# Hard-max attention on one core: dots without their pause late on, a third step in the last tiles, a larger allowance for value-row gathers, five rows ahead of the last flags

## The chip, the cores and the metric

The kernel runs on one core of one Trainium2 chip. The metric is device time in microseconds, 443.18 us before the change (median of three, 442.71 to 443.21). The profile is of one execution with a span of 441.9 us, and its times count from the start of the span. The five engines are PE (matrix), ACT (scalar), DVE (vector), POOL (GpSimd, which here issues nearly all gathers) and SP (which issues stores).

## The reference

```python
# q, k, v: (4, 4096, 128) float32
logits = np.matmul(q, k.transpose(0, 2, 1))
best = np.argmax(logits, axis=-1)
b_idx = np.arange(q.shape[0])[:, None]
return v[b_idx, best, :].astype(np.float32)
```

For each of 16384 query rows the kernel finds the key with the largest dot product, and returns that key's row of v.

## The kernel before

**Tiles.** There are 4 batches of 32 query tiles, T = 128 tiles of 128 queries. A loop over `it` handles them in a software pipeline. The order of instructions on each engine is written out by hand (a manual schedule), so each engine runs its list in the order in which the Python code emits it.

**Screen.** For each tile PE forms scores of groups of four keys in fp16, with ACT turning two 1024-wide blocks into absolute values (A, L234) and one into integers (E, L247). The DVE `fold` (L260) joins the blocks into W, which carries a group index in its low bits, and `top` (L264) takes the eight best of W. In iteration `it`, `fold` handles tile `it - 1` and `top` tile `it - 2`.

**Candidates and dots.** `gather` (L271) extracts the best group of four or two tiles (cand, L276) and puts one indirect DMA per tile into the list `near_q` (kg, L282): differences of the four keys of that group. When these are issued, a generator `dots` (L290) multiplies them with the queries (prod L300), halves twice (L305, L308) and reduces (L310). A generator advances one operation per call of `step`, of which there are two in an iteration, one after `fold` and one after `top`. A yielded `("wait", 1)` makes it pause to the next iteration; `("dve",)` lets it go on at the next step. Tiles below 108 go in groups of four, later ones in groups of two.

**Picks and rows.** When all dots of a chunk (eight tiles, four from tile 96 on) are there, `pick` (L313) finds which of the four keys wins. Its last operation is win (L333). `put_values` (L337) then puts one gather per tile (vr from v, L342) into the list `late_q`, and behind each four a store to the output (L346), which SP issues.

**The issue of gathers.** At the end of each iteration `issue` (L743) sends to POOL first what is due of `near_q`, then one of the list `fast` (gathers of the flag check), and then rows of `late_q` as long as an allowance `room` lasts. That grows by `rate` per iteration, is capped at 3, and is lowered by what was issued and by loads (`busy`).

**The end.** After the loop come the last dots and picks. `flags_last` (L466) recomputes exactly the few queries whose screen was too close: DVE makes the list of rows (row_e, L509), POOL issues `LATE` of the waiting value rows (L515), then gathers three groups of keys and the query (FK, FQ, L512); DVE computes exact dots (L594) and the winner xw_fe (L607). The other waiting rows go out by `late(1 << 20)` (L531), then the gather FV of the exact winner's row (L540), and last the scatter of FV to the output (L541), which must come after all stores to it. An earlier check of the same kind, `flag_segment` (L358), handles the first half of the tiles inside the loop.

Of the kernel before, what the change touches and what calls it, by code (L numbers as in the profile page):

```python
# [21 lines left out]
TAU = 8.0  # L22
NEAR = 0.5
SLOTS = 6
LATE = 4
NKG = 6


# [1 line left out]
def kernel(ctx, tc, q, k, v, out):  # L30
# [5 lines left out]
    T = B * NQT  # L36
# [34 lines left out]
    def put_k(b, h):  # L71
        if b >= B:
            return
        src = natk[b % 2][:, h].rearrange("p (g f) d -> p g f d", f=4)
        nc.vector.tensor_tensor(out=kd[:, h], in0=src[:, :, 1:4, :], in1=src[:, :, 0:1, :].to_broadcast([P, 4, 3, P]),
                                op=OP.subtract)
        kb16 = k16[b].rearrange("(h p n) d -> p h (n d)", p=P, n=16)
        nc.sync.dma_start(out=kb16[:, h], in_=kd[:, h].rearrange("p g f d -> p (g f d)"))
# [10 lines left out]
    def add_rest(b, h):  # L89
        if b >= B:  # L90
            return
        src = natk[b % 2][:, h].rearrange("p (g f) d -> p g f d", f=4)
        kb16 = k16[b].rearrange("(r x) d -> r (x d)", x=4).rearrange("(h p g) (f d) -> p h g f d", h=2, p=P, f=3)
        nc.gpsimd.dma_start(out=kb16[:, h].rearrange("p g f d -> p g (f d)"), in_=src[:, :, 1:4, :].rearrange("p g f d -> p g (f d)"),
                            accum_op=OP.add)

    def load_part(b, i, n=8):
        if b >= B:
            return
        if i < 8:  # L100
            load_k(b, i // 4, i % 4 * 4, i % 4 * 4 + n)
        else:
            load_q(b, (i - 8) * NQT // 8, (i - 8 + n // 4) * NQT // 8)
# [103 lines left out]
    def turn_q(b, x, y):  # L207
        nc.sync.dma_start_transpose(out=qT[b % 2][:, x * P:y * P].rearrange("p (t r) -> p t r", r=P),
                                    in_=natq[b % 2][:, x:y, :].rearrange("p t d -> p (t d)"))
# [42 lines left out]
    def screen(t):  # L252
        dpart(t, 0)
        spart(t - 1, 0)
        dpart(t, 1)
        spart(t - 1, 1)

    def fold(t):
        E, ps = E_t.pop(t)
        nc.vector.scalar_tensor_tensor(out=W_t[t % NW].bitcast(I16)[:, 1::2], in0=ps, scalar=QSCALE, in1=E,  # L260
                                       op0=OP.mult, op1=OP.max)
# [28 lines left out]
    def dots(c, x, m):  # L290
        c0 = chunks[c][0]
        d = D_t[c % 4]
        b = x // NQT
        gap = ("wait", 1) if m == 4 and x < 200 else ("dve",)
        yield "until", lambda: ("kg", x) in done, 2 if m < 4 and x < TAIL else 1
        kg = kg_t.pop(x)
        prod = rp.tile([P, 4, 3, P], FP16, tag="prod", name=f"prod_{x}")[:, 0:m]
        h = min(m, 2)
        for i in range(0, m, h):
            nc.vector.tensor_tensor(out=prod[:, i:i + h], in0=kg[:, i:i + h],  # L300
                                    in1=natq[b % 2][:, x + i - b * NQT:x + i + h - b * NQT, :].unsqueeze(2).to_broadcast([P, h, 3, P]),
                                    op=OP.mult)
            yield gap
        p1 = rp.tile([P, 4, 3, 64], FP16, tag="p1", name=f"p1_{x}")[:, 0:m]
        nc.vector.tensor_tensor(out=p1, in0=prod[:, :, :, 0:64], in1=prod[:, :, :, 64:128], op=OP.add)  # L305
        yield gap
        p2 = rp.tile([P, 4, 3, 32], FP16, tag="p2", name=f"p2_{x}")[:, 0:m]
        nc.vector.tensor_tensor(out=p2, in0=p1[:, :, :, 0:32], in1=p1[:, :, :, 32:64], op=OP.add)  # L308
        yield "dve",
        nc.vector.tensor_reduce(out=d[:, x - c0:x - c0 + m, 1:4], in_=p2, axis=AX_X, op=OP.add)  # L310
        done.update(("dot", i) for i in range(x, x + m))
# [154 lines left out]
    def flags_last(t0, t1, ready, fill, late):  # L466
# [44 lines left out]
        def get(dst, src, idx, hi):  # L511
            nc.gpsimd.indirect_dma_start(out=dst, out_offset=None, in_=src, in_offset=IOA(ap=idx, axis=0),  # L512
                                         bounds_check=hi - 1, oob_is_err=False)

        late(LATE)  # L515
        get(FK[:, 0, :], k_flat, gb[:, 0:1], B * Sk)
# [173 lines left out]
    def ready(s, it):  # L690
        if s["until"] is not None:
            if not s["until"]():
                return False
            s["until"], s["wake"] = None, it + s["n"]
        return it >= s["wake"]

    def advance(s, it, free):
        if not (ready(s, it) or free and s["until"] is None):
            return False
        try:  # L700
            y = next(s["g"])
        except StopIteration:
            live.remove(s)
            return True
        if y[0] == "wait":
            s["wake"] = it + y[1]
        elif y[0] == "until":
            s["until"], s["n"] = y[1], y[2]
            return advance(s, it, free)
        return True  # L710

    def step(it):
        quick = it >= TAIL
        waiting = [s for s in live if s["kind"] == "dots" and ready(s, it)]
        quota = 2 if len(waiting) > 1 else 1
        again = []
        for s in list(live):
            if s["kind"] == "dots":
                if quota and advance(s, it, False):
                    quota -= 1  # L720
            elif advance(s, it, False) and (quick or s["kind"] == "flags"):
                again.append(s)
        for s in again:
            if s in live:
                advance(s, it, False)
# [3 lines left out]
    def take_late(n):  # L729
        while n > 0 and late_q:  # L730
            g = late_q.pop(0)
            n -= g not in stores
            g()
        while late_q and late_q[0] in stores:
            wait_q.append((clock[0] + 2, late_q.pop(0)))
# [3 lines left out]
    def put_out(now):  # L739
        while wait_q and wait_q[0][0] <= now:  # L740
            wait_q.pop(0)[1]()

    def issue(it):  # L743
        n = 0
        clock[0] = it
        put_out(it)
        behind = len([g for g in near_q if g not in marks]) > (2 if it >= TAIL else 4)
        while near_q and (n < 1 + behind or near_q[0] in marks or it >= T - 1):
            g = near_q.pop(0)
            n += g not in marks  # L750
            g()
        if fast and it >= rest[0]:
            fast.pop(0)()
            rest[0] = it + 2
            n += 1
        if it < 16:
            take_late(2 if n == 0 and len(late_q) > 4 else 1)
            return
        b, qt = it // NQT, it % NQT
        busy = 0.7 if qt % 2 == 0 and (10 <= qt < 18 and b + 1 < B or 18 <= qt < 26 and b + 2 < B) else 0.0  # L760
        if qt in (13, 17) and b + 1 < B:
            busy += 1.0
        rate = 2.42 if it < 72 else 2.5 if it < 100 else 2.42
        room[0] = min(room[0] + rate - busy, 3.0) - n
        for i in range(2):
            if room[0] >= 1 and late_q and it < T - 1:
                take_late(1)
                room[0] -= 1
# [20 lines left out]
    for b in range(1, B):  # L789
        x = b * NQT  # L790
        units += [(x - 1, x - NQT + (6 + 3 * i // 2 if b == 1 else 1 + 2 * i), unit_k, b, i) for i in range(16)]
    for it in range(T):
        b, qt = it // NQT, it % NQT
        if it < 8:
            load_part(1, it, 4)
        elif 10 <= qt < 18 and qt % 2 == 0:
            load_part(b + 1, qt - 2)
        elif 18 <= qt < 26 and qt % 2 == 0:
            load_part(b + 2, qt - 18)
        open_units = [u for u in units if u[1] <= it]  # L800
        if open_units:
            u = min(open_units)
            units.remove(u)
            assert it <= u[0]
            u[2](*u[3:])
        if it == 1:
            turn_q(0, 4, 8)
        if it == 40:
            nc.sync.dma_start(out=q32, in_=q[B - 1].rearrange("(p t) d -> p t d", p=P)[:, NQT - 2:NQT])
        if it in (1, 2, 3):  # L810
            turn_q(0, it * 8, it * 8 + 8)
        elif qt >= 16 and qt % 2 == 0 and b + 1 < B:
            turn_q(b + 1, (qt - 16) * 2, (qt - 14) * 2)
        if it > 0:
            screen(it)
        if it >= 1:
            fold(it - 1)
        if it == 1:
            put_k(0, 1)
        if it % NQT in (9, 13):  # L820
            put_first(it // NQT + 1, it % NQT // 13)
        if it % NQT in (13, 17):
            add_rest(it // NQT + 1, it % NQT // 17)
        step(it)
        if it >= 2:
            top(it - 2)
        step(it)
        if it >= 2:
            gathers(it - 2)
        issue(it)  # L830
# [75 lines left out]
```

## Time and profile before

| What | Value |
|---|---|
| time, median of 3 | 443.18 us |
| span of the profile | 441.9 us |
| main loop, start of the last L264 | 405.5 us |
| kg gathers L282 on POOL | 126, 1003 ns each |
| vr gathers L342 with win as index | 126, 999 ns each |
| fold L260 on DVE | 128, 1306 ns |
| L264 on DVE | 128, 1227 ns |
| landing after issue, kg and vr | 3.0 and 2.7 us (medians) |

A group line of the profile gives the line, engine, operation, the tile written and the tile read, the count, the summed busy time and the mean of one. Consecutive DVE instructions overlap a little, so the distance between their starts is shorter than the duration (1.20 against 1.31 us for the fold). A gather's bar on POOL covers its issue alone; the data land later.

From the chain of work that ended last, its lines by share of the span, and its final part (start, length, engine, what):

```profile
ACT A L234 31%; ACT E L247 6%; DVE TOP L264 4%; PE psn L225 4%; POOL vr L342 4%; PE pd L225 4%; POOL kg L282 4%; DVE W L260 4%; PE psn L244 3%; DMA vr<-in_v_dram,win 3%; DMA natk<-in_k_dram 2%; DMA out_dram<-vr 1%; DMA kg<-k,cand 1%; DVE prod L300 1%; DMA vr<-in_v_dram,win_w 1%
...
419.83 2.60 DMA FK<-in_k_dram,gb_e
422.43 5.59 DMA vr<-in_v_dram,win
429.02 1.00 POOL vr L342
430.32 1.00 POOL vr L342
431.62 3.17 DMA vr<-in_v_dram,win_w
434.88 1.82 DMA out_dram<-vr
437.46 1.25 POOLq L901
```

### The profile page before, as it was taken

How to read it: one execution, taken by the hardware profiler on the slowest of the kernel's cores; microseconds unless marked ns; L12 is line 12 of the kernel's file. 1: busy time of each engine (PE TensorE's matmuls, PEld its weight loads, DVE VectorE, ACT ScalarE, POOL GpSimd, SP SyncE). 2: the span in 40 equal slices, each digit the busy share in tenths (PEclk: the TensorE clock that was granted, in tenths of full speed). 3: DMA queues.
4: the chain of work that ended last, by engine and by line, in shares of the span. 5: the costliest groups of instructions: out<-in, count | busy, mean ns of one | idle time of the engine just before them, and what ended most of it. 6: DMA issues, size and time to landing. Idle time of an engine off the chain costs nothing.

```text
span 441.9 us, 6163 instructions
## 1 busy us (share of the span) xinstructions
PE 378.9 (86%) x1830; PEld 168.0 (38%) x1830; DVE 405.9 (92%) x734; ACT 375.6 (85%) x437; POOL 306.2 (69%) x335
## 2 busy tenths in 40 slices
PE   7999999999999999999998889999889997892100
PEld 4444444444444444444443334443333333330100
DVE  2688999999999999999999999999999999999840
ACT  2899999999999999999998889999989998892000
POOL 8413456677768786777777776777777777777673
PEclk9999999999999999999999999999999999998555
DMA  7933999463326999743336993453322332323432
GB/s 123 202 101 65 157 148 139 106 130 80 108 58 134 180 163 170 147 114 91 84 94 142 173 162 100 96 132 107 85 82 84 90 89 80 88 80 102 122 113 53
DMA packets 52868, 50.54 MB, mean 114 GB/s; under 512 B 34136, under 2 KB 40890, under 8 KB 52832
## 3 DMA queue, kind: packets, MB, share of 16 engines
q0 software_dynamic: 19072, 33.87, 39.2%
q1 hardware_dynamic: 33760, 16.26, 14.5%
q8 instruction: 14, 0.23, 0.2%
q14 instruction: 22, 0.18, 0.2%
HBM read 40.05 MB, written 14.55 MB: 124 GB/s over the span
## 4 chain that ended last, share of the span: by engine, by line
ACT 37%; issue 20%; DVE 13%; PE 12%; POOL 8%; DMA 8%; POOLq 0%; ACTq 0%; DVEq 0%; SPq 0%
ACT A L234 31%; ACT E L247 6%; DVE TOP L264 4%; PE psn L225 4%; POOL vr L342 4%; PE pd L225 4%; POOL kg L282 4%; DVE W L260 4%; PE psn L244 3%; DMA vr<-in_v_dram,win 3%; DMA natk<-in_k_dram 2%; DMA out_dram<-vr 1%; DMA kg<-k,cand 1%; DVE prod L300 1%; DMA vr<-in_v_dram,win_w 1%
## 5 line engine op out<-in xcount | busy, mean ns | idle before, releaser
L234 ACT ACTIVATE A<-pd 128x1024 f16<-128x1024 f32 x256 | 260.8, 1046 | 12.5 <-PE pd L225 12.0
L282 POOL DMA_INDIRECT kg<-k,cand x126 | 126.4, 1003 | 80.0 <-DVE cand L276 48.7
L260 DVE SCALAR_TENSOR_TENSOR W<-psn,E 128x1024 int16<-128x1024 f32 x128 | 167.1, 1306 | 7.4 <-ACT E L247 5.3
L225 PE MATMUL psn<-kT,qT 128*128 128x512 f16 x512 | 151.9, 378 | 11.4 <-ACT A L234 4.0
L225 PE MATMUL pd<-kT,qT 128*128 128x512 f16 x512 | 151.9, 379 | 8.7 <-ACT A L234 8.2
L264 DVE MAX8 TOP<-W 128x8 f32<-128x1024 f32 x128 | 157.0, 1227 | 0.0
L225 PEld LDWEIGHTS <-qT 128*128 128x128 f16 x1024 | 97.9, 97 | 151.8 <-issue 62.0
L342 POOL DMA_INDIRECT vr<-in_v_dram,win x126 | 125.9, 999 | 40.0 <-issue 36.1
L244 PE MATMUL psn<-A,identh 128*128 128x512 f16 x512 | 152.1, 378 | 0.0
L247 ACT ACTIVATE E<-psn 128x1024 int16<-128x1024 f32 x128 | 132.6, 1036 | 2.3 <-PE psn L244 1.5
L244 PEld LDWEIGHTS <-identh 128*128 128x128 f16 x512 | 49.6, 97 | 60.7
L300 DVE TENSOR_TENSOR prod<-kg,natq 128x768 f16<-128x768 f16 x63 | 34.8, 554 | 0.4 <-DMA kg<-k,cand 0.4
L205 ACT ACTIVATE kT<-uk 128x256 f16<-128x256 f32 x48 | 20.6, 429 | 1.5 <-PE uk L202 1.5
L305 DVE TENSOR_TENSOR p<-prod 128x768 f16<-128x768 f16 (+1 forms) x36 | 18.1, 502 | 0.1
L310 DVE TENSOR_REDUCE D<-p 128x12 f32<-128x384 f16 (+1 forms) x36 | 17.7, 492 | 0.1
L201 PE MATMUL uk<-identh,natk 128*128 128x128 f16 x96 | 15.8, 218 | 0.0
L484 PE MATMUL fp_e<-n_e,tri 128*128 128x1 f32 x2 | 0.6, 364 | 13.5 <-DVE n_e L482 13.5
L202 PEld LDWEIGHTS <-natk 128*128 128x128 f16 x96 | 9.3, 97 | 7.2 <-issue 5.1
L308 DVE TENSOR_TENSOR p<-p 128x384 f16<-128x384 f16 (+1 forms) x36 | 11.9, 330 | 0.1
L66 POOL DMA_DIRECT2D natk<-in_k_dram x19 | 11.3, 599 | 0.8 <-POOLq L890 0.8
L201 PEld LDWEIGHTS <-natk 128*128 128x128 f16 x96 | 9.3, 98 | 5.6
L69 POOL DMA_DIRECT2D natq<-in_q_dram x15 | 9.2, 614 | 0.0
(152 smaller groups left out, 140.1 us busy)
## 6 DMA issues: line engine op xcount, KB each, us to landing
out_dram<-vr SPq DMA_DIRECT2D x31, 256.0 KB, 2.1
natq<-in_q_dram POOLq DMA_DIRECT2D x12, 256.0 KB, 5.3
natk<-in_k_dram POOLq DMA_DIRECT2D x10, 256.0 KB, 4.5
k<-kd SPq DMA_DIRECT2D x18, 128.0 KB, 3.7
k<-natk POOLq DMA_DIRECT2D x6, 384.0 KB, 6.4
kg<-k,cand POOLq DMA_INDIRECT x126, 3.0
vr<-in_v_dram,win POOLq DMA_INDIRECT x126, 2.7
natk<-in_k_dram POOLq DMA_DIRECT2D x8, 128.0 KB, 5.7
```

The source lines that it names most:

```text
L201: nc.tensor.matmul(out=o, lhsT=natk[b % 2][:, h, 4 * m + x, :], rhs=identh, start=True, stop=False)
L205: nc.scalar.activation(out=kT[b % 2][:, c:c + 256], in_=ps, func=AF.Copy)
L225: nc.tensor.matmul(out=ps[:, n * 512:(n + 1) * 512], lhsT=qT[b % 2][:, qt * P:(qt + 1) * P], rhs=kT[b % 2][:, u * 1024 + n * 512:u * 1024 ...
L234: nc.scalar.activation(out=A, in_=ps, func=AF.Abs)
L244: nc.tensor.matmul(out=ps[:, n * 512:(n + 1) * 512], lhsT=identh, rhs=A[:, n * 512:(n + 1) * 512], start=False, stop=True)
L247: nc.scalar.activation(out=E, in_=ps, func=AF.Relu, scale=QSCALE)
L260: nc.vector.scalar_tensor_tensor(out=W_t[t % NW].bitcast(I16)[:, 1::2], in0=ps, scalar=QSCALE, in1=E, op0=OP.mult, op1=OP.max)
L264: nc.vector.max(out=TOP[:, t, :], in_=W_t[t % NW].bitcast(FP32))
L282: near_q.append(lambda j=j: nc.gpsimd.indirect_dma_start(out=kg[:, j].rearrange("p f d -> p (f d)"), out_offset=None, in_=k16[t0 // NQT], ...
L300: nc.vector.tensor_tensor(out=prod[:, i:i + h], in0=kg[:, i:i + h], in1=natq[b % 2][:, x + i - b * NQT:x + i + h - b * NQT, :].unsqueeze(2 ...
L305: nc.vector.tensor_tensor(out=p1, in0=prod[:, :, :, 0:64], in1=prod[:, :, :, 64:128], op=OP.add)
L342: late_q.append(lambda j=j: nc.gpsimd.indirect_dma_start(out=vr[:, j, :], out_offset=None, in_=v_flat, in_offset=IOA(ap=win[:, i + j:i + j ...
```

## The change

Four edits are meant to shorten the queue of value rows that is still waiting when the loop ends. Dots of tile 80 and later no longer pause a tile between operations, so that they take two steps a tile. In the last 20 iterations there is a third step. The allowance is raised by stages. And five instead of four rows go out ahead of the last flags' gathers.

```diff
-LATE = 4
+LATE = 5
...
-        gap = ("wait", 1) if m == 4 and x < 200 else ("dve",)
+        gap = ("wait", 1) if m == 4 and x < 80 else ("dve",)
...
-        rate = 2.42 if it < 72 else 2.5 if it < 100 else 2.42
+        rate = 2.45 if it < 72 else 2.65 if it < 80 else 2.45 if it < 96 else 2.6 if it < 104 else 2.45 if it < 112 else 2.6
...
         if it >= 2:
             top(it - 2)
         step(it)
+        for _ in range(1 if it >= T - 20 else 0):
+            step(it)
         if it >= 2:
             gathers(it - 2)
         issue(it)
```

## The prediction

> **What bounds the kernel now.** I read the windows first, then the waits of GpSimd, then the timeline of the end. First the busy times of the engines, as totals and in two late stretches (columns: window, length, then busy time and count of PE, PEld, DVE, ACT, POOL, then clock, DMA share, GB/s):
>
> ```profile
> PE 378.9 (86%) x1830; PEld 168.0 (38%) x1830; DVE 405.9 (92%) x734; ACT 375.6 (85%) x437; POOL 306.2 (69%) x335
> ...
> 330.00:360.00 30.00, 28.07 (x118) 11.32 (x117) 29.86 (x52) 28.70 (x31) 22.69 (x23) 1.00 0.30 83
> 360.00:390.00 30.00, 26.10 (x110) 10.47 (x109) 29.55 (x60) 25.82 (x28) 22.36 (x22) 1.00 0.32 92
> ```
>
> DVE is busy 29.86 and 29.55 of 30 us: up to the last L264 (405.5 us) the time is the sum of DVE's work. One tile costs it 1.20 us for the fold L260 plus 1.14 for L264 (start to start), and dots, candidates and picks bring four tiles to some 12.2 us. POOL looks 75% busy, but is nearly full too:
>
> ```profile
> POOL vr L342 <- issue: 7.2, 22, 0.8
> POOL kg L282 <- issue: 4.6, 15, 0.3
> POOL kg L282 <- DVE cand L276: 2.9, 5, 0.9
> ```
>
> These are POOL's waits from 347 to 405 us: 0.30 us of "issue" before each gather, so a gather occupies POOL 0.95 to 1.00 + 0.30, about 1.27 us, and true waiting for a candidate is only 2.9 us, 0.3 of each being that same gap. At 3.05 us a tile POOL fits 2.4 gathers a tile, two of which would suffice for one kg and one vr; the rest works off the backlog. And the backlog decides the end (timeline):
>
> ```profile
> 411.38 0.16 DVE L333 SCALAR_TENSOR_TENSOR win<-CNT,cand 128x4 uint32<-128x4 f32 x1
> ...
> 413.88 1.00 POOL L342 DMA_INDIRECT vr<-in_v_dram,win  x1 [0.30 <-issue]
> ...
> 417.17 1.05 POOL L512 DMA_INDIRECT FK<-in_k_dram,gb_e  x1 [2.29 <-DVE row_e L509]
> ...
> 421.13 1.00 POOL L512 DMA_INDIRECT FK<-in_k_dram,gb_e  x1 [0.31 <-issue]
> ...
> 422.43 1.00 POOL L342 DMA_INDIRECT vr<-in_v_dram,win  x1 [0.30 <-issue]
> ...
> 426.57 0.17 DVE L607 TENSOR_REDUCE xw_fe<-xl_fe 128x1 uint32<-128x12 f32 x1
> ...
> 431.62 1.00 POOL L342 DMA_INDIRECT vr<-in_v_dram,win_w  x1 [0.30 <-issue]
> 432.92 0.99 POOL L512 DMA_INDIRECT FV<-in_v_dram,xw_fe  x1 [0.30 <-issue]
> 437.69 1.02 POOL L541 DMA_INDIRECT out_dram<-FV,rowk_e  x1 [3.77 <-DMA out_dram<-vr]
> ```
>
> After the four flag gathers (417.17 to 422.1) eight value rows still stand in POOL's queue, 422.43 to 432.6, one every 1.30 us. Only then come FV (its index was ready at 426.74) and, after the last store has landed, the scatter. From 422 us on POOL is the bound. Ahead of FK it waited 2.29 us for DVE.
>
> **What the skill says.** "Perfetto Trace Analysis", section "DMA Instruction — SWDGE (GPSIMD)": a GpSimd DMA's bar ends when the descriptors are written, not when the data are there. The trace agrees: 1.00 us bars, median landing 2.7 us after issue for vr and 3.0 for kg. "DMA: Bandwidth & Descriptors", section "Anatomy of one DMA — SWDGE (gpsimd) path", gives about 2.0 us plus bytes over 436 GB/s; for a kg gather of 96 KB that makes 2.2 us, an estimate by the page, and the trace's 3.0 is what I use. No page prices the reordering itself.
>
> **The change part by part.** No instruction is added or removed; I compared the order on each engine in the two built programs. I number gathers by tile: k112 is the kg gather of tile 112, v112 its value row.
>
> *Dots without the one-tile pause (x from 80), third step in the last 20 tiles.* On DVE the same operations stand earlier. DVE is saturated, so its sum is unchanged: 0. The picks come earlier: adding up the DVE durations ahead of each L333, its win moves forward 4.1 us for the picks of tiles 80 to 103, 6.5 to 7.2 for those of 104 to 111, 3.1 for 112 to 123. The other side: dots now stand ahead of some candidates, which come 0.5 to 1.2 us later up to tile 113, at most 0.5 after it; some prods of two-tile groups also move 0.45 later. One bunching cost: single tiles now hold fold and top alone, 2.34 us, where after tile 70 none took DVE under 2.77. PE and ACT may not follow for that tile: bounded by 0 (their work of the busy tile before is waiting) and 0.4 us each time, over few tiles. I take 0.1 in all.
>
> *Allowance (2.45 to 2.65).* It lets those earlier rows go out earlier. Rows issued ahead of a gather, before and after: k108 95 and 96, k112 99 and 101, k115 103 and 105, k117 106 and 108, k118 107 and 110, k121 111 and 114, k123 114 and 116, k125 115 and 118, FK 120 and 124. Each extra row costs POOL 1.27 us; the spare time (waits above 0.30) pays it back: 0.26 before k100, 0.30 before k104, 0.56 before k112, 0.21 before k114, 0.23 before k118, 0.36 before k120, 0.49 just before k121. So POOL is late by 1.27 - 0.56 = 0.7 at k108, 2 x 1.27 - 1.12 = 1.4 at k112, 2.54 - 1.33 = 1.2 at k115 and k117, 3.81 - 1.56 = 2.25 at k118, 3.81 - 2.41 = 1.4 at k121 and k125, 2.54 - 2.41 = 0.1 at k123. Where does that wait surface? At the prod of the group. For four-tile groups nothing: k103 was issued 6.3 us, k107 6.5 us ahead of the prod that reads it. For two-tile groups the last gather is 3.7 to 4.7 us ahead, against 3.0 of landing, and one of them DVE already waited for:
>
> ```profile
> 385.67 0.56 DVE L300 TENSOR_TENSOR prod<-kg,natq 128x768 f16<-128x768 f16 x1 [0.45 <-DMA kg<-k,cand]
> ```
>
> For that one (k117, landing 4.12 us) 1.2 late less 0.45 of its prod's later place leaves 0.75 of new stall. k121: 1.4 late, less 0.45, less 0 to 0.7 of slack, leaves 0.25 to 0.95, of which the 0.75 already lost counts. A stall moves everything behind it on DVE, the later candidates, folds and the whole end, so the largest lateness counts, not the sum: 0.75 to 0.95, I take 0.9. Bounds: 0 if landings are at their 2.6 us minimum, 2.25 if one falls on the most delayed gather without slack.
>
> *LATE 5, and the four rows brought ahead of FK.* After FK there are four rows instead of eight (v124, v125 and the two of win_w). That takes 4 x 1.30 = 5.2 us out of the only chain that is left, and nothing runs beside it that would end later: FV would start at 432.92 - 5.2 = 427.7, 1.0 after its index was ready. Do the four cost FK anything? v120 to v123 need the win that DVE ends at 411.54; with 0.3 and 4 x 1.30 POOL is free for FK at 417.04, where row_e let it go at 417.17 before. They just fit, by 0.1 us, in the 2.29 us wait and in the place of the four rows that now went out earlier. v118 and v119 come ahead of 411.5 even with POOL 1.4 late (k125 at 404.64 + 1.4 = 406.0, then xk, v118, xk, v119 to 412.4): v120 could start at 412.7, and its win, 0.9 later with DVE, is there at 412.4. So FK moves with DVE, by 0.9.
>
> Sum: -5.2 + 0.9 + 0.1 = -4.2; 443.18 - 4.2 = **439.0 us**.
>
> **Rivals.** (1) *No stall at all*: slack of 0.7 and later prods swallow the lateness. For it: DVE waited 0.45 us for a kg in the whole late phase. Against it: three groups had 3.7 to 3.8 us, near their landing. 443.2 - 5.2 = 438.0. (2) *POOL overloaded*: the extra rows delay the most exposed kg by the full 2.25 us and bunching costs 0.8: 443.2 - 5.2 + 3.0 = 441.0. For it: spare time is 2.4 us against 3.8 needed at k118. (3) *A wait in place of the wait*: four rows stand ahead of FK, and if they don't fit, all four delay it by 5.2 us, so FK, exact, FV and the scatter end as before: 443.2, no change. Against it: 411.54 + 0.3 + 5.2 = 417.04. (4) *Slower*: the nine two-tile groups from k108 to k124 each lose 0.7 us, since a stalled DVE delays the next candidate, and that the next gather: 9 x 0.7 = 6.3, 443.2 - 5.2 + 6.3 = 444.3. Against it: a stall of DVE also gives POOL time to catch up.
>
> **How the numbers follow.** Forecast (438.5 to 440.0) 50%, rival 1 22%, rival 2 15%, no change 4%, slower 9%. The range 437.8 to 441.5 holds the first three but for a few cases of each. Faster 0.87, same 0.04, slower 0.09.
>
> **What would show it.** Right: four L342 after the last L512 of FK, the end from FK to the scatter about 5.2 us shorter (from 20.5 to about 15.3), the last L264 0 to 2 us later than 405.5, POOL's wait ahead of FK down from 2.29 us to well under 1, DVE waits for kg of 0.5 to 1.5 us in all. Wrong: DVE waits for kg above 3 us, FK waiting behind rows while row_e is done, or ACT and PE gaps that push the main loop by over 2 us.

## The result, and the profile after

The changed kernel takes 440.35 us (median of four, 439.86 to 440.49) against 443.1 us (median of four, one more than above, 442.71 to 443.21); the ratio is 0.9937, with a 95% interval of 0.992 to 0.9955. That is 2.75 us less, where 4.2 were forecast. In eight of the twelve runs below PE's granted clock was 0.85 to 0.93 in the mean, against 0.96 here, and all kernels, the one before too, took 508 to 548 us: of those runs I read no whole times, only DVE's work and the stretch after the last fold, in which PE has almost nothing to do.

The busy totals of the changed kernel, and its two late windows (columns as in the prediction):

```profile
PE 378.8 (87%) x1830; PEld 168.2 (38%) x1830; DVE 407.8 (93%) x734; ACT 375.5 (86%) x437; POOL 304.9 (70%) x335
...
330.00:360.00 30.00, 27.17 (x115) 11.03 (x114) 29.76 (x48) 27.43 (x29) 22.99 (x24) 1.00 0.32 92
360.00:390.00 30.00, 25.59 (x109) 10.33 (x107) 29.62 (x59) 25.78 (x28) 22.62 (x23) 1.00 0.30 88
```

DVE still has hardly a gap (29.76 and 29.62 of 30 us busy), but the same 734 instructions keep it busy 1.9 us longer (405.9 before). The start of the last L264 in the kernel before, and then in the changed one:

```profile
405.51 1.23 DVE L264 MAX8 TOP<-W 128x8 f32<-128x1024 f32 x1
```

```profile
407.53 1.23 DVE L264 MAX8 TOP<-W 128x8 f32<-128x1024 f32 x1
```

The end of the timeline of the changed kernel:

```profile
417.70 1.00 POOL L342 DMA_INDIRECT vr<-in_v_dram,win  x1 [0.30 <-issue]
...
419.12 1.05 POOL L512 DMA_INDIRECT FK<-in_k_dram,gb_e  x1 [0.41 <-DVE row_e L509]
...
424.38 1.00 POOL L342 DMA_INDIRECT vr<-in_v_dram,win  x1 [0.30 <-DMA FQ<-in_q_dram,row_e]
...
428.29 1.00 POOL L342 DMA_INDIRECT vr<-in_v_dram,win_w  x1 [0.30 <-issue]
...
429.59 1.00 POOL L512 DMA_INDIRECT FV<-in_v_dram,xw_fe  x1 [0.30 <-issue]
433.66 1.02 POOL L541 DMA_INDIRECT out_dram<-FV,rowk_e  x1 [3.08 <-DMA out_dram<-vr]
```

Four rows stand behind FK instead of eight, and POOL's wait for row_e has shrunk from 2.29 to 0.41 us. Read against the kernel before:

| Stretch of the two profiles | before | after | difference |
|---|---|---|---|
| start to the last L264 | 405.51 | 407.53 | +2.02 |
| last L264 to FK | 11.66 | 11.59 | -0.07 |
| FK to the last row issued | 14.45 | 9.17 | -5.28 |
| last row to the end | 10.26 | 9.56 | -0.70 |

The last line is the landing of the last rows and stores. It varies: the profile of before is of an execution of 443.8 us, above its median, that of after of the fastest one, 439.86. The first three lines add up to -3.3, the medians differ by -2.75, so there is no room for the fourth. So the end paid as forecast, and the main loop took 2 us back. It lost them late: the L264 of tile 79 still starts 0.33 us earlier than before (256.82 against 257.14), and from there to the last L264 the stretch is 2.34 us longer. What follows asks why.

Two views speak against a late kg. The first is the prod group of the changed kernel (last column: idle time ahead of it):

```profile
L300 DVE TENSOR_TENSOR prod<-kg,natq 128x768 f16<-128x768 f16 x63 | 34.4, 546 | 0.0
```

The second is a line of POOL's waits from 347 to 407 us (total, times, longest):

```profile
POOL kg L282 <- DVE cand L276: 3.5, 7, 1.1
```

No prod waited at all (before, one waited 0.45 us), and POOL waited for candidates more often than before (7 times, not 5). The DVE timeline shows something else. First the kernel before, then the changed one, each with a pick of four tiles:

```profile
355.79 0.16 DVE L320 TENSOR_REDUCE mx<-D 128x4 f32<-128x16 f32 x1
355.86 0.55 DVE L300 TENSOR_TENSOR prod<-kg,natq 128x768 f16<-128x768 f16 x1
356.33 0.17 DVE L323 SCALAR_TENSOR_TENSOR near<-D,mx 128x16 f32<-128x16 f32 x1
356.42 1.23 DVE L264 MAX8 TOP<-W 128x8 f32<-128x1024 f32 x1
```

```profile
385.05 0.15 DVE L320 TENSOR_REDUCE mx<-D 128x4 f32<-128x16 f32 x1
385.23 0.18 DVE L323 SCALAR_TENSOR_TENSOR near<-D,mx 128x16 f32<-128x16 f32 x1
385.44 0.17 DVE L327 TENSOR_TENSOR sel<-near,iota 128x16 f32<-128x16 f32 x1
385.65 0.17 DVE L329 TENSOR_REDUCE CNT<-sel 128x4 f32<-128x16 f32 x1
```

Before, mx costs 0.07 us from start to start, because prod, which doesn't read mx, begins under its tail; near costs 0.09. After, near reads what mx has just written: it starts 0.18 after mx, sel 0.21 after near. The bars are as long as before. "Perfetto Trace Analysis", section "Optimizing Scalar/DVE Operations", of the Trainium skill says that the fixed data-access overhead of a DVE instruction shows in the profile at about twice what it costs the engine, because the half of it that waits for the write acknowledgement overlaps with the next instruction. The trace agrees for these small instructions (0.07 to 0.09 of 0.16 us), and shows that an instruction which needs the result doesn't get that overlap: near starts 0.03 us after the bar of mx has ended. It waits for a semaphore that DVE itself raises. The wait as such is not the price, for near waits for the same semaphore in the kernel before, where mx is one instruction further back, and there it follows prod at prod's usual distance of 0.47 us.

I call such a pair dependent neighbours. Counted in the built DVE lists after tile 79, the kernel before has 12 of them, the changed one 33. 21 more at some 0.115 us are 2.4 us; the stretch grew by 2.34.

Theory D: these pairs are the 2 us. Theory P, the forecast's: extra rows on POOL hold up kg gathers. Theory B: bunched dots leave tiles in which DVE outruns PE and ACT.

### The profile page after: what moved, and what is told of

Its sections match the earlier page's. It is cut to its first block, busy times and chain, and to the rows that moved or that the text cites. A ratio compares the mean times of both kernels' runs of the same rounds, so it can differ in the third digit from the quotient of the medians.

```text
span 437.9 us, 6167 instructions
## 1 busy us (share of the span) xinstructions
PE 378.8 (87%) x1830; PEld 168.2 (38%) x1830; DVE 407.8 (93%) x734; ACT 375.5 (86%) x437; POOL 304.9 (70%) x335
## 4 chain that ended last, share of the span: by engine, by line
ACT 41%; issue 19%; DVE 16%; PE 14%; DMA 6%; POOL 3%; POOLq 0%; ACTq 0%; DVEq 0%; SPq 0%
ACT A L234 34%; ACT E L247 7%; DVE TOP L264 6%; PE psn L225 5%; PE psn L244 4%; DVE W L260 4%; PE pd L225 4%; DMA natk<-in_k_dram 2%; DMA FK<-in_k_dram,gb_e 2%; DMA out_dram<-vr 1%; DVE prod L300 1%; POOL vr L342 1%; POOL kg L282 1%; DVE p L305 1%; DVE D L310 1%
## 5 line engine op out<-in xcount | busy, mean ns | idle before, releaser
L264 DVE MAX8 TOP<-W 128x8 f32<-128x1024 f32 x128 | 155.9, 1218 | 0.0
```

The source lines that it names most:

```text
L264: nc.vector.max(out=TOP[:, t, :], in_=W_t[t % NW].bitcast(FP32))
```

## The experiments

### Parts of the change alone, and pairs without the change

**Third step alone** (kernel before):

```diff
         step(it)
+        for _ in range(1 if it >= T - 20 else 0):
+            step(it)
         if it >= 2:
             gathers(it - 2)
```

> The kernel before with only the third step in the last 20 tiles. Its queue is as before: 8 value rows stand after FK. In the DVE list after tile 79, 33 instructions read what the instruction just ahead of them wrote, as many as in the changed kernel, against 12 before. Theory D (each such pair costs DVE about 0.115 us): the last L264 starts 2.0 to 2.4 us later than before (near 407.7) and the time is 445.2, slower than before. Theory P (the main loop got longer because extra rows on POOL hold up kg gathers): no extra rows here, so 443.1 and the last L264 near 405.5. Theory B (tiles with fold and L264 alone outrun PE and ACT): the third step adds some bunching, 443.1 to 444.

A second run of it, on another chip:

> The kernel before with only the third step in the last 20 tiles, once more, since its first comparison fell on a chip that held PE's clock down and lengthened every kernel by some 80 us. Value rows as before, 8 behind FK; 33 dependent neighbours on DVE after tile 79 against 12. Theory D (such a pair costs DVE 0.115 us): last L264 near 407.7, 445.2. Theory P (extra rows on POOL hold up kg gathers): no extra rows, 443.1 and 405.5. Theory B (bunched tiles outrun PE and ACT): 443.1 to 444.

**The changed kernel without the third step**: those two lines taken out.

> The changed kernel without its third step; dots without pause from tile 80, allowance and LATE 5 stay. 12 dependent neighbours on DVE after tile 79 as before, and 6 rows after FK. Theory D: the last L264 is back near 405.5 to 405.7; the end carries two rows more than the changed kernel, 2.6 us; time 440.35 - 2.0 + 2.6 = 441.0. Theory P: two of four extra rows remain, so half of the 2 us remains; 442.0. Theory B: the bunched tiles from the missing pause remain, so up to 2 us remain; 443.0.

**Pause of the dots alone** (kernel before):

```diff
-        gap = ("wait", 1) if m == 4 and x < 200 else ("dve",)
+        gap = ("wait", 1) if m == 4 and x < 80 else ("dve",)
```

> The kernel before with only the pause of the dots taken away from tile 80 on. 12 dependent neighbours as before, 7 rows after FK instead of 8. Theory D: main loop as before (last L264 near 405.5), one row less at the end, 443.1 - 1.3 = 441.8. Theory B: tiles of fold and L264 alone appear here as in the changed kernel; last L264 1 to 2 us later, 443 to 444. Theory P: one extra row, within POOL's spare time, 441.8.

**Picks in a row** (kernel before), dependent neighbours without any other part of the change:

```diff
         nc.vector.tensor_reduce(out=mx[:, :, 0], in_=d, axis=AX_X, op=OP.max)
-        yield "dve",
...
         nc.vector.tensor_reduce(out=CNT[:, t0:t1], in_=sel, axis=AX_X, op=OP.add)
+        yield "dve",
+        yield "dve",
+        yield "dve",
         done.add(("cnt", c))
```

(the yields behind near and sel are taken away too)

> The kernel before with the first four operations of each pick (mx, near, sel, CNT) put in a row, and the freed steps placed after them, so that win stays where it was: the same DVE work, the same gathers, 8 rows after FK. Dependent neighbours: 39 instead of 12 after tile 79 and 31 instead of 5 before it. Theory D: 27 x 0.115 = 3.1 us more in the late part, and where DVE is the bound in the early part too, up to 26 x 0.115 = 3.0 more: 446.2 to 449.2. Theories P and B: nothing they speak of changes, 443.1 within 0.5.

All five are among the eight runs of which I read no times, so the expected times were not tested. (How far such times go apart: the third step alone took 0.986 of the time of the kernel before in one run and 1.014 in the other.) What they do show is DVE's busy time, in order of the number of dependent neighbours, in the late and the early part. Three runs that are described further below, of the same eight, belong into the same table:

| Kernel | late, early pairs | DVE busy |
|---|---|---|
| pause alone | 12, 5 | 410.1 |
| changed, without third step | 12, 5 | 410.5 |
| LATE 8 alone (below) | 12, 5 | 411.0 |
| changed, other third step, two runs (below) | 18, 5 | 411.6, 411.3 |
| third step alone, two runs | 33, 5 | 412.6, 412.8 |
| picks in a row | 39, 31 | 415.8 |

From the page of the pause alone and that of the picks in a row, with equal instructions:

```profile
PE 399.7 (78%) x1830; PEld 171.9 (33%) x1830; DVE 410.1 (80%) x734; ACT 380.4 (74%) x437; POOL 301.5 (58%) x335
```

```profile
PE 405.5 (76%) x1830; PEld 173.9 (33%) x1830; DVE 415.8 (78%) x734; ACT 382.4 (72%) x437; POOL 302.0 (57%) x335
```

Three kernels with equal counts differ by up to 0.9 us. Against them 6 more pairs add 0.3 to 1.5 us, 21 more add 1.6 to 2.7, 53 more add 4.8 to 5.7: for the two larger numbers that is 0.08 to 0.13 us each, whichever edit made them. Whether that becomes time depends on DVE being the bound, which it was not here. That needed another design.

### With DVE made the bound by force

Two further maxima a tile over the previous W, written to a scratch tile that nobody reads:

```diff
                                        op0=OP.mult, op1=OP.max)
+        for _ in range(2):
+            if t > 0:
+                nc.vector.max(out=TOPX, in_=W_t[(t - 1) % NW].bitcast(FP32))
```

DVE then needs over 5 us a tile, and POOL has spare time. (The kernel before took 529.6 us on the chip of these two runs, but between 445 and 700 us the views of both show no wait of DVE for any other engine or transfer.) The base and the third step alone:

> The kernel before with DVE made the bound by force: behind each fold two more L264-like maxima over the previous W go to a scratch tile, about 2 x 1.14 us a tile more, so that DVE needs some 5.3 us a tile, PE and ACT far less, and POOL has much spare time. All theories: 443 + 127 x 2.28 = 733 us, the base for the run beside it.

> The same forced DVE bound, with the third step in the last 20 tiles. POOL can't delay a kg gather here (theory P) and PE and ACT can't be outrun (theory B), so both expect the time of the run beside it, 733. Theory D (a DVE instruction that reads what its neighbour just wrote costs about 0.115 us more): 21 more such pairs, 2.0 to 2.4 us more than the run beside it.

Measured: 740.16 us (739.6 to 740.89) and 742.47 (742.26 to 742.8), 2.31 us apart; both are some 7 to 9 us above the 733 that was worked out for the base. From the L264 of tile 79 (the line is L268 here) to the last one it is 259.56 and 262.45 us. The last one in the base, and then with the third step:

```profile
701.86 1.21 DVE L268 MAX8 TOP<-W 128x8 f32<-128x1024 f32 x1
```

```profile
704.54 1.21 DVE L268 MAX8 TOP<-W 128x8 f32<-128x1024 f32 x1
```

The first lines of the two pages:

```profile
PE 427.1 (58%) x1830; PEld 171.7 (23%) x1830; DVE 702.4 (95%) x988; ACT 399.4 (54%) x437; POOL 300.0 (41%) x335
```

```profile
PE 427.6 (58%) x1830; PEld 171.8 (23%) x1830; DVE 704.7 (95%) x988; ACT 399.3 (54%) x437; POOL 299.3 (40%) x335
```

DVE's busy time grows by 2.3 us, the median time by as much: 2.31 / 21 = 0.11 us a pair. In the two profiled executions, which are 3.0 us apart, the stretch grew by 2.89, 0.14 a pair, of which 0.03 are short gaps between DVE's bars. Neither a late kg nor a waiting PE can have done that, as POOL is busy 40% and PE 58% and DVE waits for neither. Theory D holds; P and B are out for the third step.

The next two are the whole change, and the change with a third step that avoids such pairs. For this, the generator that moved last is remembered, and the third step moves only one generator, which must be another:

```diff
+        moved[0] = s
         try:
             y = next(s["g"])
...
+    moved = [None]
...
+    def other(it):
+        for s in list(live):
+            if s is not moved[0] and advance(s, it, False):
+                return
...
-        for _ in range(1 if it >= T - 20 else 0):
-            step(it)
+        if it >= T - 20:
+            other(it)
```

> The changed kernel under the forced DVE bound (two more maxima a tile). Theory D: against the forced version of the kernel before (740.2) the main loop grows by the dependent pairs, +2.3 as with the third step alone, and the end loses four rows behind FK, -5.2: 737.3. Theories P and B: POOL has spare time and PE and ACT are not outrun, so only -5.2: 735.0.

> The same with the third step that moves only a generator which was not the last to move: 18 dependent neighbours after tile 79 instead of 33, the same 4 rows behind FK. Theory D: 15 x 0.11 = 1.7 us less than the run beside it, 735.6. Theories P and B: equal to it.

Measured: 737.13 (737.06 to 737.43) and 735.95 (735.17 to 736.71). The changed kernel is 3.0 us under the forced base, as D had it; these two ran on another chip than the base, but all four reach the L264 of tile 79 at 442.1 to 442.4. From there to the last L264 the changed kernel takes 262.31 us, nearly as long as the third step alone, and the other third step 260.44. Of these 1.87 us the medians show 1.18, and the two profiled executions only 0.68: in them the end, from FK on, took 20.03 instead of 18.88.

### The other third step in the plain kernel, and the rows alone

> The changed kernel with another third step: it advances only one generator, and none that was the last to move, so that the operation it emits seldom reads what stands just ahead of it. 18 dependent neighbours on DVE after tile 79 instead of 33; the rows as in the changed kernel, 4 behind FK. Theory D: 15 x 0.115 = 1.7 us less in the main loop (last L264 near 405.9), of which POOL, which then has less time ahead of FK, takes some back; 440.35 - 1.7 + 0.4 = 439.0. Theories P and B: extra rows and bunching stay, 440.3.

> The changed kernel with a third step that moves only a generator which was not the last to move (18 dependent neighbours on DVE after tile 79 instead of 33, 4 rows behind FK as in the changed kernel), once more, since its first comparison fell on a chip that held PE's clock down. Theory D: main loop 1.2 (as under the forced DVE bound) to 1.7 us shorter than in the changed kernel, of which POOL, with less time ahead of FK, takes up to 0.6 back: 439.0 to 439.6. Theories P and B: 440.3.

Both runs are among the eight, so it stays open whether this version beats the changed kernel. They also had an odd end: FK to the end took 21.05 and 21.23 us with four rows behind FK, and this wait is from the stretch after the last fold of the first run (total, times, longest):

```profile
DVE xp_fe L594 <- DVE xd_fe L594: 3.3, 5, 1.1
```

DVE stood still between dots, up to 1.1 us at a time. When their gathers landed is not in this trace, so late data are not ruled out for these waits; but DVE also stood still for 0.6 us ahead of n_e (L524), which reads only what DVE had just written. The forced version of the same change had none of this. The cause is open.

**Eight rows ahead of the last flags, nothing else** (kernel before): `LATE = 4` becomes `LATE = 8`.

> The kernel before with LATE 8 alone: 124 rows ahead of FK and 4 behind, as in the changed kernel, but nothing else brought forward. POOL ends its fourth row at 414.9, four more take 5.2 us, so FK starts at 420.4 instead of 417.2: 3.2 us later, and 5.2 us less behind it: 442.9 - 2.0 = 440.9. If rows ahead of FK merely change places with it: 442.9. If POOL has room for all four: 437.7. The main loop as before under theory D (last L264 near 405.5).

This run is one of the eight too, and DVE stood still in its end as well, 4.7 us in all ahead of row_e, so that FK's wait is not that of an undisturbed run:

```profile
500.98 1.00 POOL L342 DMA_INDIRECT vr<-in_v_dram,win  x1 [0.30 <-issue]
504.17 1.01 POOL L512 DMA_INDIRECT FK<-in_k_dram,gb_e  x1 [2.19 <-DVE row_e L509]
```

But POOL's own part is plain: it was free for FK at 500.98 + 1.30 = 502.28, 14.5 us after the last L264 (487.79), where FK started 11.66 after it in the kernel before. So rows that are only put ahead of FK would delay it by about 2.8 us, and give back half of what they save; this is worked out, not measured as a time.

What nearly all runs measured alike, but for the two odd ends above, is the price of a row behind FK, from FK to the end:

| Rows behind FK | FK to end, us |
|---|---|
| 8 (before; third step alone, twice; picks in a row; two forced) | 24.7; 25.1, 24.5; 24.2; 24.1, 24.6 |
| 7 (pause alone) | 23.1 |
| 6 (changed without third step) | 21.7 |
| 4 (changed; two forced; LATE 8) | 18.7; 18.9, 20.0; 19.0 |

That is about 1.4 us a row, 1.30 of it POOL's issue.

One thing follows for the third step. Without it (6 rows behind FK instead of 4) FK starts 12.07 us after the last L264 instead of 11.59, and FK to the end takes 21.7 us instead of 18.7. So the third step earns some 3.4 us at the end and costs 2.3 in the main loop: nearly all that the dependent neighbours cost is its own price. Its net gain of about 1 us or less is worked out from single profiles, not measured as a time.

## Why the prediction was right, and where not

**Rows behind FK, -5.2: right.** FK to the last row is 5.28 us shorter, and the table above shows the same slope in LATE 8, which has nothing else of the change.

**"They just fit": right.** The last of the four rows begins at 417.70, so POOL is free at 419.0, and row_e ends at 419.10. What it would have cost without the earlier dots and the allowance is worked out from LATE 8 alone: some 2.8 us.

**"DVE is saturated, so its sum is unchanged: 0": the step that failed.** The number of instructions is unchanged, the sum is not. I took over the prices of the old order, as start-to-start distances, and did not ask what such a distance rests on. In the new order 21 more instructions read their neighbour's result. That term, put at 0, measures +2.3 us after tile 79 in the profiles, although the 0.45 us wait for k117 is gone there too, and +2.3 in the medians under the forced bound.

**"I take 0.9" for POOL's lateness: wrong in its cause.** No prod waited for a kg. The ledger of extra rows was right as an order, but it held the candidates at their old times. They came later with DVE, and POOL caught up: k112 was issued 0.27 us after its candidate, as in the kernel before, not 1.4 late. The sign that the prediction named for this term, DVE waits for kg of 0.5 to 1.5 us in all, did not appear: there were none. That this 0.9 lay on the right side is luck, as the measured +2.0 has another cause; without it the forecast would have been 438.1, 2.25 us too low. The total lies in the wide range, but above the forecast's own 438.5 to 440.0.

**Bunching 0.1: nothing seen.** Folds 2.31 and 2.33 us apart occur, and no wait of DVE for PE or ACT is recorded from tile 79 on. Under the forced bound, where PE and ACT can't matter, the third step alone gives the whole +2.3.

The sum was -5.2 + 1.0 = -4.2; with the term as measured it is -5.2 + 2.3 = -2.9, against -2.75 of the medians. Rival 2's time, 441.0, was nearest, but its mechanism, a delayed kg, was not seen.

## What to carry to other kernels

On an engine without gaps, reordering isn't free: take the price of an instruction from a place in the profile with the same kind of neighbour, and count in the new order how many read what stands just ahead of them. A chain of small operations wants something independent between each two; a scheduler that lets one generator move twice in a row removes just that. And when a queue stands behind a late event, work taken from behind it pays in full only where it fits into time that the queue's engine spends waiting ahead of it.

## What I had not expected of the hardware

A DVE instruction of 0.16 us on 16 elements per partition costs 0.07 to 0.09 us beside independent neighbours and 0.18 to 0.21 if the next one needs it; a dot's first halving (0.34 us, 384 wide) 0.26 and 0.38. The difference, 0.10 to 0.13 us, was the same for reductions, products and comparisons, and in runs with a mean PE clock of 0.90 and of 0.96. Nearly all of it appears as busy time, the rest as gaps of about 0.03 us, and no view lists it as a wait. The standing DVE in the ends of three runs, up to 1.8 us at a time, is unexplained; all three are among the eight runs with the lower clock.
